# Products that nobody reads beside the copies in the recurrence of an RWKV-7 scan

## The chip, the cores and the metric

The kernel runs on one core of a Trainium2 chip. The metric is the device time of one execution in microseconds, as the median of several runs. A core has a matrix engine (TensorE, in the profile PE, with its weight loads as PEld), three engines for elementwise work (VectorE or DVE, ScalarE or ACT, GpSimd or POOL), SyncE (SP), whose queue starts transfers, and DMA engines. TensorE's output goes to PSUM, from where the elementwise engines read it.

## What is computed

A two-layer encoder on 256 tokens and 16 learned ones ahead of them, 1024 features, with 32-bit products. Layer 0 is differential attention and a dense SwiGLU; layer 1 an RWKV-7 time mixing in both directions and a SwiGLU with eight experts, of which each token takes two. The change concerns the scan of layer 1, cut here from the reference:

```python
def _wkv7_step(S, inp):
    r, w, k, v, kk, a = inp
    sa = jnp.einsum('bhvk,bhk->bhv', S, kk)
    S = S * w[:, :, None, :] - sa[..., None] * (kk * a)[:, :, None, :] + v[..., None] * k[:, :, None, :]
    y = jnp.einsum('bhvk,bhk->bhv', S, r)
    return S, y
...
_, y_fwd = lax.scan(_wkv7_step, S0, (r_t, tm(decay[0]), tm(kd[0]), v_t, kk_t, tm(a[0])))
_, y_bwd = lax.scan(_wkv7_step, S0, (r_t, tm(decay[1]), tm(kd[1]), v_t, kk_t, tm(a[1])), reverse=True)
...
out = ((y + bonus.reshape(B, L, D)) * g).astype(x.dtype)
return jnp.einsum('bld,de->ble', out, w_o)
```

There are 16 heads of 64 features; the state S of a head is 64x64.

## The kernel before

The scan is computed in chunks of 64 tokens, four chunks in each direction. The 16 heads go as eight pairs (f = 0 to 7); one head of a pair lies in the lower 64 partitions (LO), the other in the upper 64 (HI). For each pair these parts run, in `rwkv`:

- `rv` (L718) projects the pair's r and v. `prep` (L764 on) makes the decays, the rates and the matrices between the tokens of a chunk: X, TK, GA. `inverse` (L913 on) solves a triangular system for each of the eight chunks: 15 rounds on VectorE over 16x16 blocks (a shuffle L930, a product L931, a sum L932), then two levels of products (L946, L953, L967, L978, L980); its result is TF. `values` (L906) sets in the values.
- `chain` (L986 on) is the recurrence. A start (L1011 to L1020) takes the 16 learned tokens; then come four steps, i = 0 to 3, each with forward chunk i and backward chunk 3 - i. A step: products of X with the state R to slot 0 of a PSUM tile `pc` (L1028) and to the result `py` (L1032); a copy W of slot 0 on ScalarE (L1037); scaled states Zk on ScalarE (L1042); products of TF with W to slot 1 (L1045); copies of slot 1 to R, half of each direction on ScalarE (L1048) and half on VectorE (L1049); products of TK with R to slot 2 (L1054, not in step 3) and of GA with R to `py` (L1056); and on VectorE the next state from slot 2 and Zk (`state`, L1005 or L1007, not in step 3). A step needs the state of the step before it.
- `norm` (L1063 on) normalizes `py`, turns it (L1082) and multiplies by the gate, which gives gT. `out_proj` (L1171) multiplies gT with the output weights; the products of pairs 0 to 5 and the residual stand in the last two pairs, each tied behind a named product of the recurrence (the list `order`).

A tile `pc` has slots 0 to 3 of 64 columns for each direction: `psum.tile([128, 2, 4, 64], F32, name=f"pc{f % 2}", bufs=1)`, so pairs of even and odd number have one each, of one PSUM bank. Slot 3 is unused.

The order of the instructions of an engine is set by a scheduler, from the order of the program, the dependences, its own estimate of durations and priorities; the recurrence is programmed under a raised priority (`CHAIN_PRIORITY = 100`). Preparation and inverses of later pairs are set around the recurrence of an earlier one, and the last step of a pair can share its time with the first of the next. Where an instruction reads a PSUM tile that another engine has written, it waits for that engine. After the scan come a norm, the router and the experts, which stream their weights from memory.

Of the kernel before, what the change touches and what calls it, by code (L numbers as in the profile page):

```python
# [29 lines left out]
RANKS = (0, 5, 1, 2, 6, 3, 4, 7)  # L30
PLACES = {'W': 128, 'N': 64}
NL = 7
# [62 lines left out]
class Trunk:  # L95
# [193 lines left out]
    def attention(self, ap_, psum, xT, xh, xl, oh, ol, fill):  # L289
# [30 lines left out]

        raws, W = {}, {}

        def weights(h, i):
            if h % 2 == 0:
                raws[i] = self.load(w_in, 0, NF, i * D + h * 128, 256, 3 * D)
            c0 = (h % 2) * 128
            W[h, i] = self.parts(raws[i][:, :, c0:c0 + 128])

# [3 lines left out]
        def project(h, i, ks):  # L332
            if ks[0] == 0:
                S[h][i] = psum.tile([128, T], F32, name="pj", bufs=2)
            wh, wl = W[h, i]
            for k in ks:
# [271 lines left out]
    def projections(self, lp):  # L608
# [5 lines left out]
        temp = lambda f: pool.tile([128, T], F32, name="ln_q", bufs=LQ) if f % 2 else None  # L614
        W = []

        def weights(c):
            raw = self.load(I['rw_w_rkv'], D, NF, c * 256, 256, D)
            W.extend(self.parts(raw[:, :, j * 128:j * 128 + 128]) for j in range(2))

# [122 lines left out]
    def scan_consts(self, sp):  # L743
# [14 lines left out]
        for t in self.BK + self.X[0:2]:  # L758
            nc.vector.memset(t, 0.0)

    def bank(self, psum, tag="pi"):
        return psum.tile([128, 512], F32, name=tag, bufs=1 + (tag == "pa"))

# [222 lines left out]
    def chain(self, sp, psum, f, S):  # L986

        nc = self.nc
        xm, rm, R, tkm = self.xm[f % 3], self.rm[f % 2], S['R'], S['tkm']
        LO, HI = slice(0, 64), slice(64, 128)  # L990
        heads = ((0, LO), (1, HI))
        pend = S['pend']
        Zk = [None, None]
        S['order'] = order = []

        def steps():
            ps = psum.tile([128, 2, 4, 64], F32, name=f"pc{f % 2}", bufs=1)
            return [ps[:, d] for d in range(2)]

        def state(d, c, pc, keep):  # L1000

            for h, s in heads:
                e = pend[s, d, keep:keep + 1]
                if Zk[d] is None:
                    nc.vector.tensor_scalar(R[s, c, d, h, :], pc[s, 2, :], e, None, op0=OP.mult)  # L1005
                else:
                    nc.vector.scalar_tensor_tensor(R[s, c, d, h, :], pc[s, 2, :], e, Zk[d][s], op0=OP.mult, op1=OP.add)  # L1007


        pc = steps()[0]  # L1010
        nc.tensor.matmul(pc[LO, 0, :], xm[HI, 0, 0:64], rm[HI, 0, :], start=True, stop=True)  # L1011
        nc.tensor.matmul(pc[HI, 0, :], xm[LO, 1, 64:128], rm[LO, 1, :], start=True, stop=True)
        wm = sp.tile([128, 64], F32, name="wm", bufs=1)
        nc.scalar.copy(wm, pc[:, 0, :])
        for s in (LO, HI):
            nc.tensor.matmul(pc[s, 1, :], S['Tm'][s, :], wm[s, :], start=True, stop=True)
        nc.scalar.copy(rm[LO, 0, :], pc[LO, 1, :])
        nc.vector.tensor_copy(rm[HI, 1, :], pc[HI, 1, :])
        for h, s in heads:
            nc.tensor.matmul(pc[s, 2, :], tkm[:, h, :], rm[:, h, :], start=True, stop=True)  # L1020
        state(0, 0, pc, 4)
        py = self.bank(psum, f"py{f % 2}")[:, :256].rearrange("p (c j) -> p c j", c=4)
        for i in range(4):
            cs = (i, 3 - i)
            pcs = steps()
            for d in range(2):
                for h, s in heads:
                    nc.tensor.matmul(pcs[d][s, 0, :], S['X'][d][:, cs[d], 192 * h:192 * h + 64], R[:, cs[d], d, h, :],  # L1028
                                     start=True, stop=True)
            for d in range(2):  # L1030
                for h, s in heads:
                    last = nc.tensor.matmul(py[s, cs[d], :], S['X'][d][:, cs[d], 64 + 64 * h:128 + 64 * h], R[:, cs[d], d, h, :],  # L1032
                                            start=i == 0 and d == 0, stop=False)
            order.append(last)
            W = sp.tile([128, 2, 64], F32, name="W")
            for d in range(2):
                nc.scalar.copy(W[:, d, :], pcs[d][:, 0, :])  # L1037
            for d in range(2):
                if i < 3 and (i or not d):
                    Zk[d] = sp.tile([128, 64], F32, name=f"Zk{d}")  # L1040
                    for h, s in heads:
                        nc.scalar.activation(Zk[d][s], R[s, cs[d], d, h, :], AF.Copy, scale=pend[s, d, cs[d] - d:cs[d] - d + 1])  # L1042
            for d in range(2):
                for h, s in heads:
                    last = nc.tensor.matmul(pcs[d][s, 1, :], S['TF'][:, 4 * d + cs[d], h, :], W[:, d, :], start=True, stop=True)  # L1045
            order.append(last)
            for d in range(2):
                nc.scalar.copy(R[LO, cs[d], d, 0, :], pcs[d][LO, 1, :])  # L1048
                nc.vector.tensor_copy(R[HI, cs[d], d, 1, :], pcs[d][HI, 1, :])  # L1049
            for d in range(2):  # L1050
                c = cs[d]
                if i < 3:
                    for h, s in heads:
                        nc.tensor.matmul(pcs[d][s, 2, :], S['TK'][d][:, c, h, :], R[:, c, d, h, :], start=True, stop=True)  # L1054
                for h, s in heads:
                    last = nc.tensor.matmul(py[s, c, :], S['GA'][d][:, c, h, :], R[:, c, d, h, :], start=False, stop=i == 3 and d == 1)  # L1056
            order.append(last)
            if i < 3:
                for d in range(2):
                    state(d, cs[d] + 1 - 2 * d, pcs[d], cs[d] - d)  # L1060
        return py
# [454 lines left out]
    def moe(self, ep, psums, scanp):  # L1516
# [3 lines left out]
        with tc.tile_pool(name="wsp", bufs=WS) as self.wsp, ExitStack() as ps:  # L1520
# [5 lines left out]
            ring = [chunk(self.wraw, n=2048)] * 3  # L1526
            once = [chunk(mp, m, n, bufs=1) for m, n in (("ymoe", 2048), ("hth", FT), ("htl", FT), ("xe1", 2048))]
            self.raws = chain(first[:-1], once[1:3], first[-1:], once[:1], ring[:2], once[3:], ring[2:], cycle(first + ring))
            psums.close()
            psum = ps.enter_context(tc.tile_pool(name="moep", bufs=1, space=PSUM))  # L1530
# [205 lines left out]
```

## Time and profile before

| | us |
|---|---|
| median of 3 runs | 1870.36 |
| lowest and highest | 1864.54 and 1871.2 |
| profiled execution | 1868.09 |
| its span on the core | 1866.0 |
| TensorE busy in the span | 1704.3 |
| VectorE busy in the span | 1275.7 |
| scan, from the first start to the last R copy | 551 to 859.3 |

The rows are of one execution. A row of the timeline has the start, the time, the engine, the line, the operation with its names, and how many instructions it merges; in brackets stands how long the engine had been idle and what released it. A 64-wide product of 32-bit numbers is two records (passes) of TensorE. The granted clock (PEclk) is a share of full speed, 2.4 GHz; 0.50 is 1.2 GHz.

### The profile page before, as it was taken

Reading aid. Unit: us, or ns where it says so; the run is one execution under the profiler, and the core shown is the slowest. Engines: PE = TensorE matmul, PEld = TensorE weight load, DVE = VectorE, ACT = ScalarE, POOL = GpSimd, SP = SyncE. Lnnn points to the kernel's source line nnn. Section 1 sums busy time; section 2 is a strip of 40 time slices with the busy share of each in tenths; the row PEclk is TensorE's granted clock in tenths of the full one; section 3 lists DMA queues with packets and bytes.
Section 4 is the critical chain, followed back from the end, with each engine's and each line's share of the span. In section 5 each row is a group of like instructions: output and inputs, shape, how many; then the busy total and the mean of one; then the engine's idle time right before and its main releaser. Section 6 shows DMA issues by size and latency. Waiting matters only on the chain.

```text
span 1866.0 us, 30513 instructions
## 1 busy us (share of the span) xinstructions
PE 1704.3 (91%) x11422; PEld 1362.5 (73%) x11422; DVE 1275.7 (68%) x2135; ACT 912.2 (49%) x1612; POOL 624.8 (33%) x551
## 2 busy tenths in 40 slices
PE   6998999987988888897999999999999999999995
PEld 6887999975666666676986567888856668888542
DVE  6885755587868886854896446989934469899332
ACT  5665444455335335533674235766723356777210
POOL 4233100166545544512353112544501125445101
PEclk9999999988878878897999999999999999999998
DMA  6331555531101000355769899998999999999991
GB/s 210 112 114 46 179 171 178 173 102 47 57 24 53 24 24 2 131 204 207 245 235 347 347 425 426 425 343 306 341 357 353 422 420 350 322 326 348 395 388 78
DMA packets 130737, 431.79 MB, mean 231 GB/s; under 512 B 13689, under 2 KB 78674, under 8 KB 130578
## 3 DMA queue, kind: packets, MB, share of 16 engines
q1 hardware_dynamic: 127202, 427.78, 61.4%
q10 hardware_dynamic: 3376, 1.95, 0.4%
q8 instruction: 92, 1.51, 0.3%
q14 instruction: 67, 0.55, 0.1%
HBM read 428.66 MB, written 1.05 MB: 230 GB/s over the span
## 4 chain that ended last, share of the span: by engine, by line
PE 36%; issue 5%; DVE 4%; DMA 3%; POOL 1%; ACT 1%; SPq 0%; DVEq 0%; POOLq 0%; ACTq 0%
PE pgu L1414 14%; PE pgu L1429 6%; PE pd L135 3%; PE pdn L1478 3%; PE pd L136 3%; PE pd L134 3%; DVE w_lo L127 2%; DMA w_raw<-in_moe_w_down_dram 1%; POOL w_lo L127 1%; DMA w_raw<-in_moe_w_up_dram 1%; DMA w_raw<-in_moe_w_gate_dram 1%; DVE hid L1610 1%; PE pd L1508 1%; PE pt L1359 1%; PE pt L1445 1%
## 5 line engine op out<-in xcount | busy, mean ns | idle before, releaser
L127 DVE TENSOR_TENSOR w_lo<-w_raw,w_hi 128x896 fp32r<-128x896 f32 (+2 forms) x445 | 648.8, 1497 | 152.4 <-ACT w_hi L124 145.3
L124 ACT CAST w_hi<-w_raw 128x896 fp32r<-128x896 f32 (+2 forms) x580 | 537.2, 960 | 277.1 <-PE pd L136 70.9
L127 POOL TENSOR_TENSOR w_lo<-w_raw,w_hi 128x1024 fp32r<-128x1024 f32 (+1 forms) x135 | 335.3, 2484 | 624.1 <-ACT w_hi L124 476.3
L1414 PE MATMUL pgu<-w_hi,xe 128*128 128x448 f32 x1280 | 299.6, 369 | 2.4 <-DVE hid L1610 1.6
L1414 PEld LDWEIGHTS pgu<-w_hi,xe 128*128 128x128 f32 x1280 | 237.4, 188 | 26.7 <-issue 6.5
L1414 PE MATMUL pgu<-w_lo,xe 128*128 128x448 f32 x640 | 164.5, 369 | 4.7 <-DVE w_lo L127 4.6
L1429 PE MATMUL pgu<-w_raw,xs 128*64 128x448 f32 x768 | 158.1, 544 | 0.0
L1414 PEld LDWEIGHTS pgu<-w_lo,xe 128*128 128x128 f32 x640 | 118.5, 188 | 18.9 <-DVE w_lo L127 8.1
L135 PE MATMUL pd<-w_lo,hth 128*128 128x512 f32 (+1 forms) x320 | 121.3, 384 | 10.0 <-DVE w_lo L127 6.3
L136 PE MATMUL pd<-w_hi,htl 128*128 128x512 f32 (+1 forms) x320 | 119.7, 375 | 0.0
L1429 PEld LDWEIGHTS pgu<-w_raw,xs 128*64 128x64 f32 x768 | 59.1, 136 | 81.0 <-issue 76.9
L134 PE MATMUL pd<-w_hi,hth 128*128 128x512 f32 (+1 forms) x320 | 101.3, 376 | 4.1 <-ACT w_hi L124 4.1
L135 PEld LDWEIGHTS pd<-w_lo,hth 128*128 128x128 f32 x320 | 62.3, 195 | 28.9 <-DVE w_lo L127 8.3
L1478 PE MATMUL pdn<-w_raw,hth 128*64 128x512 f32 (+1 forms) x384 | 79.6, 542 | 0.0
L134 PEld LDWEIGHTS pd<-w_hi,hth 128*128 128x128 f32 x320 | 58.9, 194 | 17.3 <-ACT w_hi L124 5.7
L136 PEld LDWEIGHTS pd<-w_hi,htl 128*128 128x128 f32 x320 | 62.1, 194 | 10.2 <-issue 0.7
L134 PE MATMUL pj<-xh,w_hi 128*128 128x272 f32 x192 | 58.5, 305 | 9.8 <-ACT w_hi L124 4.9
L1478 PEld LDWEIGHTS pdn<-w_raw,hth 128*64 128x64 f32 x384 | 32.5, 137 | 37.8 <-issue 30.4
L136 PE MATMUL pj<-xh,w_lo 128*128 128x272 f32 x192 | 56.7, 295 | 0.6 <-DVE w_lo L127 0.6
L135 PE MATMUL pj<-xl,w_hi 128*128 128x272 f32 x192 | 56.5, 294 | 0.0
L1618 DVE TENSOR_TENSOR hid<-hid,pgu 64x896 f32<-64x896 f32 x12 | 13.0, 1091 | 62.3 <-ACT hid L1616 62.3
L153 POOL COPY ln_s<-ln_y 128x272 f32<-128x272 f32 x2 | 0.8, 412 | 156.2 <-DVE ln_y L150 156.2
(634 smaller groups left out, 3570.6 us busy)
## 6 DMA issues: line engine op xcount, KB each, us to landing
w_raw<-in_moe_w_down_dram SPq DMA_DIRECT2D x128, 896.0 KB, 7.5
w_raw<-in_moe_w_gate_dram SPq DMA_DIRECT2D x126, 896.0 KB, 7.3
w_raw<-in_moe_w_up_dram SPq DMA_DIRECT2D x126, 896.0 KB, 6.9
w_raw<-in_attn_w_in_dram SPq DMA_DIRECT2D x12, 1024.0 KB, 9.3
w_raw<-in_rw_w_rkv_dram SPq DMA_DIRECT2D x12, 1024.0 KB, 5.0
w_raw<-in_ffn_w_gate_dram SPq DMA_DIRECT2D x11, 1024.0 KB, 6.9
w_raw<-in_ffn_w_up_dram SPq DMA_DIRECT2D x11, 1024.0 KB, 5.3
w_raw<-in_ffn_w_down_dram SPq DMA_DIRECT2D x8, 1024.0 KB, 5.3
```

Source lines behind the costliest of these rows:

```text
L124: nc.scalar.copy(hi, raw)
L127: self.parted = eng.tensor_tensor(lo, raw, hi.bitcast(F32), op=OP.subtract)
L134: mm(ps, wh, xh, start=start, stop=False)
L135: mm(ps, wh, xl, start=False, stop=False)
L136: return mm(ps, wl, xh, start=False, stop=stop)
L1359: nc.tensor.matmul(ps[:, j, :], self.h3[:, t, 128 * f:128 * f + 128], G['og'][:, t, :], start=t == 0, stop=t == 1)
L1414: mm(ps[a][:, b, :448], xe[:, x, k, :], w[:, 448 * b:448 * b + 448], start=k == 0 and i == 0, stop=k == NF - 1 and i == 2)
L1429: self.tc.keep_in_program_order(self.nc.tensor.matmul(ps[a][64 * h:64 * h + 64, b, :448], xs[:, k, :], raws[h][:, o:o + 448], start=k == 0 ...
L1445: nc.tensor.transpose(pt[:, j, :], s[:, i0 + j:FT:NB], self.ident)
L1478: self.tc.keep_in_program_order(self.nc.tensor.matmul(pd[64 * q:64 * q + 64, c:c + n], h[:, i, :], raw[:, o:o + n], start=first and i == 0 ...
L1508: nc.tensor.matmul(ps, os, x, start=i == 0, stop=i == len(Y[q]) - 1)
L1610: nc.vector.tensor_tensor(cols(a), cols(a), pu[a][:, :, :448], op=OP.mult)
```

## The change

A helper `warm` issues n products of the constant identity matrix with itself, 64 columns wide, into a place in PSUM. Each step's `pc` tile gives its unused slot, of direction 1, lower half, as that place. Four such products are programmed behind the products with X, ahead of the copy W, and eight behind the products with GA, ahead of the next state (none in step 3). That is 8 x (4 x 4 + 3 x 8) = 320 products, 640 passes. Nothing reads them.

```diff
--- before.py
+++ after.py
@@ -758,6 +758,11 @@
         for t in self.BK + self.X[0:2]:
             nc.vector.memset(t, 0.0)
 
+    def warm(self, ps, n):
+
+        for _ in range(n):
+            self.nc.tensor.matmul(ps, self.ident[:, 0:ps.shape[0]], self.ident[:, 0:ps.shape[1]], start=True, stop=True)
+
     def bank(self, psum, tag="pi"):
         return psum.tile([128, 512], F32, name=tag, bufs=1 + (tag == "pa"))
 
@@ -992,9 +997,11 @@
         pend = S['pend']
         Zk = [None, None]
         S['order'] = order = []
+        spare = []
 
         def steps():
             ps = psum.tile([128, 2, 4, 64], F32, name=f"pc{f % 2}", bufs=1)
+            spare[:] = [ps[LO, 1, 3, :]]
             return [ps[:, d] for d in range(2)]
 
         def state(d, c, pc, keep):
@@ -1032,6 +1039,7 @@
                     last = nc.tensor.matmul(py[s, cs[d], :], S['X'][d][:, cs[d], 64 + 64 * h:128 + 64 * h], R[:, cs[d], d, h, :],
                                             start=i == 0 and d == 0, stop=False)
             order.append(last)
+            self.warm(spare[0], 4)
             W = sp.tile([128, 2, 64], F32, name="W")
             for d in range(2):
                 nc.scalar.copy(W[:, d, :], pcs[d][:, 0, :])
@@ -1055,6 +1063,7 @@
                 for h, s in heads:
                     last = nc.tensor.matmul(py[s, c, :], S['GA'][d][:, c, h, :], R[:, c, d, h, :], start=False, stop=i == 3 and d == 1)
             order.append(last)
+            self.warm(spare[0], 8 if i < 3 else 0)
             if i < 3:
                 for d in range(2):
                     state(d, cs[d] + 1 - 2 * d, pcs[d], cs[d] - d)
```

Behind the helper all lines of the scan move: L1028 is L1035 in the changed kernel, L1032 L1039, L1037 L1045, L1045 L1053, L1049 L1057, L1054 L1062, L1056 L1064, L1005 and L1007 L1012 and L1014, L930 to L932 L935 to L937, L1171 L1180, and the new products are L764. The scheduler sets the whole order anew, so other instructions move too. Three places follow.

TensorE in a step of the last pair, before (`pi` is the output projection, `pc` and `py` are the tiles of the step):

```order
L1032 MATMUL py_9207<-R,X_4978 64x64 x2
L1032 MATMUL py_9207<-R,X_4979 64x64
L1028 MATMUL pc_9281<-R,X_4978 64x64 x2
L1028 MATMUL pc_9281<-R,X_4979 64x64 x2
L1032 MATMUL py_9207<-R,X_4979 64x64
L1171 MATMUL pi<-w_raw,gT 128x256 x2
L1045 MATMUL pc_9281<-W,w_raw 64x64 x4
L1171 MATMUL pi<-kT,gT 128x256
L1056 MATMUL py_9207<-R,GA 64x64 x3
```

and in the changed kernel, with the new products at L764:

```order
L1039 MATMUL py_9487<-R,X_4979 64x64
L1035 MATMUL pc_9585<-R,X_4978 64x64 x2
L1035 MATMUL pc_9585<-R,X_4979 64x64 x2
L1039 MATMUL py_9487<-R,X_4979 64x64
L764 MATMUL pc_9585<-blob_61 64x64
L1180 MATMUL pi<-w_raw,gT 128x256
L764 MATMUL pc_9585<-blob_61 64x64
L1180 MATMUL pi<-w_raw,gT 128x256
L764 MATMUL pc_9585<-blob_61 64x64 x2
L1053 MATMUL pc_9585<-W,w_raw 64x64 x4
L1180 MATMUL pi<-kT,gT 128x256
L1064 MATMUL py_9487<-R,GA 64x64 x3
```

Four new products stand between the products with R and those with W, among the passes of the output projection, and before the next step eight more stand behind the products with TK and GA. The copy W and the state wait for the last of them.

TensorE at the seam of pairs 6 and 7, before: the start of pair 7 (L1011 to L1020) and its first step, `pc_9208`, stand behind the last products of pair 6, `py_8982`:

```order
L1056 MATMUL py_8982<-R,GA 64x64 x4
L1171 MATMUL pa<-kT,gT 128x256 x2
L1171 MATMUL pf<-kT,gT 128x256 x2
L906 MATMUL pi<-blob_61,vT 64x64 x10
L1011 MATMUL pc_9194<-rm_4973,xm 64x64
L1082 MATMUL pc_9129<-blob_61,Y 64x64 x8
L1012 MATMUL pc_9194<-rm_4973,xm 64x64
L1016 MATMUL pc_9194<-wm,Tm 64x64 x2
L1020 MATMUL pc_9194<-rm_4973,tkm 64x64 x2
L1032 MATMUL py_9207<-R,X_4978 64x64
L1028 MATMUL pc_9208<-R,X_4978 64x64 x2
L1028 MATMUL pc_9208<-R,X_4979 64x64 x2
```

and in the changed kernel, where `py_9222` and `pc_9370` belong to step 3 of pair 6, and `py_9487` and `pc_9488` to step 0 of pair 7:

```order
L1035 MATMUL pc_9370<-R,X_4976 64x64 x2
L1035 MATMUL pc_9370<-R,X_4977 64x64 x2
L1039 MATMUL py_9222<-R,X_4977 64x64
L764 MATMUL pc_9370<-blob_61 64x64
L1180 MATMUL pa<-kT,gT 128x256
L1039 MATMUL py_9487<-R,X_4978 64x64
L1035 MATMUL pc_9488<-R,X_4978 64x64 x2
L1035 MATMUL pc_9488<-R,X_4979 64x64 x2
L1039 MATMUL py_9487<-R,X_4978 64x64
L1039 MATMUL py_9487<-R,X_4979 64x64 x2
L764 MATMUL pc_9488<-blob_61 64x64 x4
```

Both steps now stand within each other. The same holds at the seams of pairs 2 and 3 and of 3 and 4; in the kernel before, the seams 0/1, 1/2, 5/6 and in part 4/5 were like this already.

VectorE around the state behind step 2 of pair 5 (`pc_8702` before), beside the inverse of pair 7 (`TD`, `inv_b`; the last number of a shape tells the round: 128x9x15 is the last):

```order
L1049 COPY R<-pc_8702 64x64
L932 TENSOR_TENSOR TD<-TD,inv_b 128x9x5
L930 STREAM_SHUFFLE inv_b<-TD 128x9x6
L931 TENSOR_TENSOR inv_b<-inv_b,QD 128x9x6
L1018 COPY rm_4972<-pc_8969 64x64
L1007 SCALAR_TENSOR_TENSOR R<-pc_8702,pend,Zk_8714 64x64 x2
L1007 SCALAR_TENSOR_TENSOR R<-pc_8702,pend,Zk_8717 64x64 x2
L932 TENSOR_TENSOR TD<-TD,inv_b 128x9x6
L1005 TENSOR_SCALAR R<-pc_8969,pend 64x64 x2
L930 STREAM_SHUFFLE inv_b<-TD 128x9x7
L931 TENSOR_TENSOR inv_b<-inv_b,QD 128x9x7
L932 TENSOR_TENSOR TD<-TD,inv_b 128x9x7
```

and in the changed kernel, where that state reads `pc_8926`:

```order
L1057 COPY R<-pc_8926 64x64
L937 TENSOR_TENSOR TD<-TD,inv_b 128x9x14
L1025 COPY rm_4972<-pc_9209 64x64
L935 STREAM_SHUFFLE inv_b<-TD 128x9x15
L1057 COPY R<-pc_8926 64x64
L936 TENSOR_TENSOR inv_b<-inv_b,QD 128x9x15
L937 TENSOR_TENSOR TD<-TD,inv_b 128x9x15
L1012 TENSOR_SCALAR R<-pc_9209,pend 64x64 x2
L947 STREAM_TRANSPOSE inv_s<-T_9101 128x512
L1014 SCALAR_TENSOR_TENSOR R<-pc_8926,pend,Zk_8942 64x64 x2
L1014 SCALAR_TENSOR_TENSOR R<-pc_8926,pend,Zk_8945 64x64 x2
```

Before, the state stood within round 6 of that inverse; now it stands behind round 15. On SP's queue two loads of expert weights pass one load of the output weights; behind the scan a few neighbours change places.

## Rows read from the trace of the kernel before

**Rows 1.** The page's head:

```profile
span 1866.0 us, 30513 instructions
```

**Rows 2.** The chain of waits that ended last, of 700 to 900 us:

```profile
0 pieces in order of time: start us, us, what
```

**Rows 3.** Engines by stretch: stretch, length, busy times, granted clock, DMA share, GB/s:

```profile
core 0: us, PE busy (x) PEld busy (x) DVE busy (x) ACT busy (x) POOL busy (x), PEclk, DMA share, GB/s
...
551.00:796.90 245.90, 207.73 (x2534) 161.72 (x2534) 195.41 (x674) 111.52 (x354) 118.00 (x193) 0.83 0.14 49
796.90:859.30 62.40, 59.26 (x659) 46.67 (x659) 27.32 (x107) 21.30 (x76) 5.27 (x8) 0.87 0.41 161
...
680.00:690.00 10.00, 9.83 (x87) 8.24 (x88) 9.47 (x38) 2.22 (x8) 5.69 (x10) 0.50 0.00 0
```

**Rows 4.** Timeline of 849.6 to 855.4 us, a step of pair 7:

```profile
850.03 0.28 PE L1056 MATMUL py<-R,GA 128*64 128x64 f32 x2
...
850.24 1.23 DVE L1007 SCALAR_TENSOR_TENSOR R<-pc,pend,Zk 64x64 f32<-64x64 f32 x4 [0.56 <-PE pc L1054]
...
851.62 0.45 PE L1028 MATMUL pc<-R,X 128*64 128x64 f32 x8
...
852.11 0.33 ACT L1037 COPY W<-pc 128x64 f32<-128x64 f32 x2
...
852.12 1.13 PE L1171 MATMUL pi<-w_raw,gT 128*128 128x256 f32 x4
...
853.18 0.45 PE L1045 MATMUL pc<-W,w_raw 128*64 128x64 f32 x8
...
854.75 0.45 PE L1054 MATMUL pc<-R,TK 128*64 128x64 f32 x8
...
855.25 0.28 DVE L1007 SCALAR_TENSOR_TENSOR R<-pc,pend,Zk 64x64 f32<-64x64 f32 x1 [0.56 <-PE pc L1054]
```

**Rows 5.** Timeline of 834 to 848.5 us, the start of pair 7:

```profile
834.79 0.33 PE L1011 MATMUL pc<-rm,xm 64*64 64x64 f32 x2 [0.94 <-DVE rm L909]
...
836.86 0.33 PE L1016 MATMUL pc<-wm,Tm 64*64 64x64 f32 x4 [0.67 <-ACT wm L1014]
...
837.75 0.48 PE L1020 MATMUL pc<-rm,tkm 128*64 128x64 f32 x4 [0.56 <-DVE rm L1018]
...
838.61 0.47 PE L1032 MATMUL py<-R,X 128*64 128x64 f32 x2 [0.38 <-DVE R L1005]
...
839.02 0.70 PE L1028 MATMUL pc<-R,X 128*64 128x64 f32 x8
...
846.40 1.84 PE L1171 MATMUL pi<-w_raw,gT 128*128 128x256 f32 x4
```

**Rows 6.** Timeline of TensorE, one pass by itself at full clock:

```profile
813.27 0.22 PE L1056 MATMUL py<-R,GA 128*64 128x64 f32 x1
```

**Rows 7.** Waits in the scan: us in total, times, longest:

```profile
ACT W L1037 <- PE pc L1028: 15.5, 12, 5.1
...
DVE R L1007 <- PE pc L1054: 6.9, 7, 2.7
DVE gsm L875 <- PE pa L874: 6.8, 3, 3.0
```

**Rows 8.** Timeline of 634 to 638.5 us, a state in the first part:

```profile
635.19 0.45 PE L1054 MATMUL pc<-R,TK 128*64 128x64 f32 x8
...
638.02 0.59 DVE L1007 SCALAR_TENSOR_TENSOR R<-pc,pend,Zk 64x64 f32<-64x64 f32 x2
```

**Rows 9.** Groups of VectorE in the scan: count, busy us, mean ns, idle before:

```profile
L932 DVE TENSOR_TENSOR TD<-TD,inv_b 128x9 f32<-128x9 f32 (+14 forms) x90 | 27.1, 301 | 2.3
L931 DVE TENSOR_TENSOR inv_b<-inv_b,QD 128x9 f32<-128x9 f32 (+14 forms) x90 | 25.5, 284 | 2.4
...
L930 DVE STREAM_SHUFFLE inv_b<-TD 128x9 f32<-128x9 f32 (+14 forms) x90 | 22.2, 247 | 0.8
```

## The prediction

> **What bounds the kernel now.** I read first the page's head, then the chain of waits, then the stretches by engine, then single steps. The profiled execution took 1868.09 us, 2.1 us of it outside its span [rows 1], and lies 2.3 us under the median of the three runs (1870.36). The chain that ended last has no piece in 700 to 900 us [rows 2]: it begins in the experts, which need the router and so the result of the last head pair. The scan stands before that, from 551 to 859.3 us, and what makes it longer or shorter moves the rest one to one. It has two parts [rows 3]. In the first 245.9 us VectorE works 195.4 us and TensorE 207.7: recurrence, preparation of later pairs and the inverses run side by side, neither engine is full, and the recurrence waits now for one, now for the other. In the last 62.4 us TensorE works 59.3 and VectorE 27.3: the recurrence of pairs 6 and 7 and the output projection (L1171) share a nearly full TensorE. The granted clock is 0.83 and 0.87 there. In single microseconds it stands at 1.00 or 0.50, so about (1 - 0.83) x 2 = 34% of the first part, 83.6 us, ran at the lower level (1.2 GHz), such as 680 to 690 us.
>
> One step of the last pair is 5.0 us [rows 4]: state (L1007) at 850.24, products with R, copy W at 852.11, products with W at 853.18, R copies, TK products at 854.75, next state at 855.25. Between the copy W and the products that read it TensorE does four passes of L1171, so this wait is no hole in this part. Holes stand only at the start of pair 7 [rows 5], 0.94, 0.67, 0.56 and 0.38 us, and the clock is low behind them: eight passes L1028 take 0.70 us at 839.02 against 0.45 at 851.62, four of L1171 1.84 at 846.40 against 1.13 at 852.12 [rows 4, 5].
>
> **The price of a spare product.** A product is two passes of 64 columns. No such product exists before, so the nearest rows bound it. Passes that alternate between the two halves cost (0.45 - 0.22) / 7 = 0.033 us each; the second pass to the same half adds 0.28 - 0.22 = 0.06 [rows 4, 6]. All spares write the same 64 partitions, so I take 0.06, or 0.12 us a product: 0.48 us for the four, 0.96 for the eight, 38.4 us for all 320. The ends are 21 us (0.033) and, at the lower clock with the ratio 0.70 / 0.45, 60 us. Nobody reads them, but they lie in the PSUM tile of their step: the changed program's copy W waits for the last of the four and the state for the last of the eight. So they do not run during the copy; they stand ahead of it. Behind the copy W wait ACT's Zk copies, and behind the state whatever VectorE has queued.
>
> The Trainium skill, PSUM — Partial Sum Buffer, section "PSUM bank collisions raise a hardware error", asks that PSUM be guarded by bank and quadrant and not by address, so a copy may not pass a matmul to other columns of its bank. The changed order agrees; no run here shows a collision. Were the guard by address, the felt share of the spares in the first part below would be near 0 instead of 9.4.
>
> **The last 62.4 us.** 84 of the spares stand here (4 for step 3 of pair 5, 40 each for pairs 6 and 7). TensorE is full, so they count in full: 84 x 0.12 = +10.1 (at 0.033 a pass 5.5). The change also lets step 0 of pair 7 share a step with step 3 of pair 6. By path alone that would save a whole step; but the output projection that fills those steps stays and TensorE has no room, so only the holes go: 0.94 + 0.67 + 0.56 + 0.38 = -2.5. If the clock no longer falls at 838, the 9.6 us to 848.2 shrink by a ratio of about 0.63 (0.45 / 0.70 and 1.13 / 1.84): -3.5. The other low stretch of this part, (1 - 0.87) x 2 x 62.4 - 10 = 6 us, would give 2.3 by the same ratio; I take half, -1.2. Sum: **+2.9**; ends about -2 (cheap spares, both falls gone) and +12 (clock as before, one hole left).
>
> **The first 245.9 us.** 236 spares, 28.3 us.
> - What of them is felt: the state waited for the TK products 7 times of 24, the copy W for its products 12 times of 32 [rows 7]; elsewhere VectorE or ACT came later than TensorE. At 635.19 the TK products begin, 0.45 us long, and the state runs at 638.02 [rows 8]: 2.4 us of slack for 0.96 of spares. I take a third: +9.4 (0 to 28.3).
> - The inverse of pair 7: ten of its fifteen rounds (L930 to L932) stood behind state 2 of pair 5 on VectorE and now stand ahead of it. A round is (27.1 + 25.5 + 22.2) / 90 = 0.83 us [rows 9], ten are 8.3. VectorE is idle a fifth of this part, spread in small pieces; I take half on the path: +4.1 (0 to 8.3).
> - Two further seams (pairs 2/3 and 3/4) share a step. 20 serial steps lie in this part, 12.3 us each, of which VectorE works 9.8 (195.4 / 20). Its work stays, so a step less saves its idle 2.5: 2 x -2.5 = -5 (0 to -25).
> - The clock: TensorE is busy 84% of the 83.6 us at the lower level, 70 us, which at the ratio 0.63 would be 44: 26 us less of TensorE's work. VectorE is late as often as not, so a third of that would be felt, 8.7; that most falls go, not all, makes it -7 (0 to -26).
>
> Sum: **+1.5**. The transfers move little (on SP's queue two expert loads pass one load of the output weights, with DMA share 0.14 in this part [rows 3]): 0. If the loads were late, the first product of the output projection would wait, and 62.4 us of work stand behind it.
>
> **Forecast.** +2.9 + 1.5 = +4.4 on 1868.09 is 1872.5. It is set against a median that stands 2.3 above this execution, but whose own runs spread over 6.7 us; I say 1873. A difference under 0.5% (9.35 us) is about what a measurement of this kernel can't tell from no change.
>
> **Rivals.**
> 1. Slower: the spares as a new wait in every step. In the first part they are felt in full where the VectorE work between R copies and state no longer covers TensorE's answer; it decides once that cover falls under the 0.96 us of the eight. For it: 12 copies W and 7 states wait for TensorE already, and rounds of pair 7's inverse, which could have served as cover behind state 5.2, move ahead. Against: slack of 2.4 us as in [rows 8]. Price: 28.3 + 10.1 - 2.5 + 4.1 - 5 = +35, with no gain from the clock: about 1903; with two thirds felt 1894. Chance 0.27.
> 2. Faster: the clock stays up. TensorE has more passes around each wait, and neither part runs at 1.2 GHz. Last part: 10.1 - 2.5 - 3.5 - 2.3 = +1.8. First part, if all 26 us are felt, since VectorE itself waits for preparation products in slow stretches (L874's 6.8 us in three waits, [rows 7]): -26 + 9.4 + 4.1 - 5 = -17.5. Together -15.7, 1852; with the seams worth more, 1840. Against: the falls come in waits for R copies and for rm [rows 5], and no spare stands there; the spares are done before the copy starts. Chance 0.23.
> The Trainium skill, TensorE: Matmul & The Clock Gate, section "HAM oscillation — how this bites in real kernels", says that a kernel whose bursts of matmuls are parted by waits has its clock taken back in each wait and starts every burst slow. The low clock behind the holes of [rows 5] agrees; by that rule alone the outcome would be this rival's 1852.
> 3. The change does not do what it says: it adds passes, the falls stay where they are, and the spares hide behind VectorE and in the new seams. Last part 10.1 - 2.5 = +7.6, first part -5 + 4.1 + a little, near +7 together or less: 1866 to 1876. Chance 0.08, within 0.5%.
>
> **How the numbers follow.** The forecast has 0.42, its own range 1860 to 1885: 0.05 of it lies above and 0.05 under the 0.5%. Faster 0.23 + 0.05 = 0.28, slower 0.27 + 0.05 = 0.32, same 0.32 + 0.08 = 0.40. For 8 in 10 the range reaches into both rivals, to rival 2's 1852 and a little under, and past the two thirds of rival 1: 1850 to 1897. It is no wider since TensorE's extra work is bounded at 38.4 us at the upper clock, and the freed time at 26 + 6.
>
> **What would show it.** In the profile after: 640 passes more on TensorE at L764, mean distance 0.06 us; copies W that start right behind the last of four, and states behind the last of eight; a last part with no hole at the start of pair 7 and 62 to 67 us long; granted clock over 0.87 in the first part and near 1.00 in the last; DVE's waits for the TK products up from 7 to about 12, by under 1 us each. I am wrong if the clock in the first part is over 0.95 with a scan under 295 us (rival 2), or if the waits of state and copy W grow by 20 us and more in sum (rival 1); also if the last part shortens by more than 2 us, which would mean that TensorE's rate there, not its passes, was the limit.

## The result, and the profile after

The changed kernel takes 1885.26 us in the median of four runs (1883.59 to 1887.04), against 1870.78 for the kernel before in the same comparison; the ratio is 1.0097, with a 95% interval of 1.0073 to 1.0121. It is slower, by 0.7% to 1.2%. The forecast of 1873 was no change; the range of 1850 to 1897 holds the time, and it lies at the very upper end of the forecast's own 1860 to 1885.

The profiled execution took 1886.28 us, its span is 1884.1, 18.1 more than before [rows 1]. The page's head and its group of the new products (lines, engine, count, busy us, mean ns):

```profile
span 1884.1 us, 31806 instructions
PE 1733.3 (92%) x12062; PEld 1390.2 (74%) x12062; DVE 1280.1 (68%) x2135; ACT 913.5 (48%) x1612; POOL 631.3 (34%) x551
...
L764 PE MATMUL pc<-blob 128*64 128x64 f32 x640 | 59.4, 245 | 0.0
```

The 640 passes are there. The scan now ends at 876.8 us instead of 859.3, and behind it nothing changed by more than a microsecond. The engines by stretch in the changed kernel, with the cut at the state behind step 2 of pair 5, as in [rows 3]:

```profile
core 0: us, PE busy (x) PEld busy (x) DVE busy (x) ACT busy (x) POOL busy (x), PEclk, DMA share, GB/s
...
551.00:811.30 260.30, 236.99 (x3027) 190.38 (x3028) 207.08 (x716) 112.98 (x356) 120.63 (x196) 0.86 0.17 60
811.30:876.80 65.50, 63.60 (x816) 49.88 (x811) 19.25 (x68) 20.73 (x74) 3.78 (x6) 1.00 0.29 102
```

The last part grew from 62.4 to 65.5 us, the first from 245.9 to 260.3: most of the loss is in the first part, though 1.1 of its 14.4 us pass before the first state has ended (552.5 us, before 551.4). VectorE has 11.7 us more to do there (207.08 against 195.41), most of it the pulled-ahead inverse of pair 7: in the last part it has 8.1 less (19.25 against 27.32). The granted clock rose in both parts, from 0.83 to 0.86 and from 0.87 to 1.00, and the kernel is slower all the same. The waits that answer to [rows 7], us in total, times, longest:

```profile
ACT W L1045 <- PE pc L764: 24.3, 17, 6.3
...
DVE R L1014 <- PE pc L764: 16.4, 10, 2.8
```

Copy W and state no longer wait for the products that they read but for the new ones behind them; 15.5 + 6.9 = 22.4 us became 40.7. What such a wait is made of shows a step of the last pair, in the timeline of the changed kernel:

```profile
864.50 0.45 PE L1035 MATMUL pc<-R,X 128*64 128x64 f32 x8
...
865.00 0.70 PE L1180 MATMUL pi<-w_raw,gT 128*128 128x256 f32 x2
865.63 0.33 PE L764 MATMUL pc<-blob 128*64 128x64 f32 x2
865.89 0.70 PE L1180 MATMUL pi<-w_raw,gT 128*128 128x256 f32 x2
866.52 0.45 PE L764 MATMUL pc<-blob 128*64 128x64 f32 x4
867.00 0.33 ACT L1045 COPY W<-pc 128x64 f32<-128x64 f32 x2 [2.13 <-PE pc L764]
...
868.95 0.45 PE L1062 MATMUL pc<-R,TK 128*64 128x64 f32 x8
869.24 0.28 PE L1064 MATMUL py<-R,GA 128*64 128x64 f32 x2
869.45 1.13 PE L1180 MATMUL pi<-kT,gT 128*128 128x256 f32 x4
870.51 1.15 PE L764 MATMUL pc<-blob 128*64 128x64 f32 x16
871.70 1.23 DVE L1014 SCALAR_TENSOR_TENSOR R<-pc,pend,Zk 64x64 f32<-64x64 f32 x4 [2.80 <-PE pc L764]
```

The products with R start at 864.50; before, the copy W came 0.49 us behind them (851.62 to 852.11, [rows 4]), now it comes at 867.00, 2.5 us behind. It waits not only for the four new products, half a microsecond, but for the passes of the output projection that stand between them in TensorE's queue. Those used to run beside the copy. The same at the state: the TK products start at 868.95, the state at 871.70, 2.75 us later where it was 0.50 (854.75 to 855.25).

### The profile page after: what moved, and what is told of

It reads as the page before. It is cut to its first block, busy times and chain, and to the rows that moved or that the text cites. A ratio compares the mean times of both kernels' runs of the same rounds, so it can differ in the third digit from the quotient of the medians.

```text
span 1884.1 us, 31806 instructions
## 1 busy us (share of the span) xinstructions
PE 1733.3 (92%) x12062; PEld 1390.2 (74%) x12062; DVE 1280.1 (68%) x2135; ACT 913.5 (48%) x1612; POOL 631.3 (34%) x551
## 3 DMA queue, kind: packets, MB, share of 16 engines
q1 hardware_dynamic: 127202, 427.78, 61.1%
HBM read 428.66 MB, written 1.05 MB: 228 GB/s over the span
## 5 line engine op out<-in xcount | busy, mean ns | idle before, releaser
L1423 PEld LDWEIGHTS pgu<-w_lo,xe 128*128 128x128 f32 x640 | 118.5, 188 | 18.8 <-DVE w_lo L127 8.1
L134 PE MATMUL pj<-xh,w_hi 128*128 128x272 f32 x192 | 58.6, 305 | 12.5 <-ACT w_hi L124 5.1
L764 PE MATMUL pc<-blob 128*64 128x64 f32 x640 | 59.4, 245 | 0.0
L764 PEld LDWEIGHTS pc<-blob 128*64 128x64 f32 x640 | 50.7, 157 | 6.5 <-issue 5.0
```

The lines of the kernel that those rows point to most:

```text
L134: mm(ps, wh, xh, start=start, stop=False)
L764: self.nc.tensor.matmul(ps, self.ident[:, 0:ps.shape[0]], self.ident[:, 0:ps.shape[1]], start=True, stop=True)
L1423: mm(ps[a][:, b, :448], xe[:, x, k, :], w[:, 448 * b:448 * b + 448], start=k == 0 and i == 0, stop=k == NF - 1 and i == 2)
```

## The experiments

Each engine's queue can be held to a given order: between every two neighbours of the wanted order a dependence is set that orders the issue and waits for nothing. So the new products and the new order, which came together, can be taken apart. All runs below but `before` and `after` are held in this way; the kernel before held to its own order was not run, so what the hold itself costs is known only together with an order.

```diff
+def in_order(tc):
...
+    dep = mybir.DependencyInfo(mybir.DependencyClass.NoSync, mybir.DependencyReason.DATA)
+    for name, text in ORDER.items():
...
+        for a, b in zip(places[:-1], places[1:]):
+            tc.add_manual_dep(mine[b], mine[a].name, dep, reason="order")
...
 def trunk(tc, I, out, dbg=None):
     Trunk(tc, I, out, dbg).build()
+    in_order(tc)
```

All times are ratios to the kernel before on the same chip, since its median differed between the three sets of runs: 1869.1 us beside order_only, spares_only, off_after and off_before, 1865.3 beside only_four, only_eight, doubled and inverse_back, 1862.2 beside the other four. Its single runs spread from 1857 to 1876 us, so one profiled execution shows where time goes, not by how much a kernel is slower to a few microseconds. "Scan" is the length from the end of the first state to the end of the last R copy in the run's one profile, "waits" the waits of copy W and state for products that stand in their PSUM tile or new ones, "clock" the granted one in the scan.

| run | new products | ratio (95%) | scan, us | waits, us | clock |
|---|---|---|---|---|---|
| before | 0 | 1 | 307.8 | 22.4 | 0.84 |
| after | 320 | 1.0097 (1.0073 to 1.0121) | 324.3 | 40.7 | 0.89 |
| order_only | 0 | 1.0002 (0.9989 to 1.0015) | 307.6 | 12.5 | 0.85 |
| spares_only | 320 | 1.0065 (1.0046 to 1.0083) | 321.5 | 51.3 | 0.88 |
| off_after | 320 | 1.0049 (1.0032 to 1.0066) | 314.2 | 15.8 | 0.91 |
| off_before | 320 | 1.0053 (1.0031 to 1.0074) | 314.8 | 20.8 | 0.89 |
| only_four | 128 | 1.0035 (1.0015 to 1.0055) | 307.9 | 34.5 | 0.86 |
| only_eight | 192 | 1.0070 (1.0039 to 1.0101) | 311.8 | 37.3 | 0.89 |
| doubled | 640 | 1.0222 (1.0193 to 1.0251) | 343.4 | 77.8 | 0.93 |
| inverse_back | 0 | 1.0012 (0.9988 to 1.0036) | 303.2 | 9.7 | 0.85 |
| best_order | 0 | 1.0019 (1.0000 to 1.0038) | 302.3 | 13.1 | 0.87 |
| holes | 256 | 1.0064 (1.0045 to 1.0082) | 313.5 | 26.5 | 0.89 |
| best_holes | 256 | 1.0086 (1.0058 to 1.0115) | 316.4 | 18.8 | 0.90 |
| first_pairs | 240 | 1.0056 (1.0036 to 1.0076) | 310.5 | 40.0 | 0.89 |

One caution goes with the table. The kernel before was traced once, in the execution of 1868.09 us. For `after` and the first set, the ratios and the differences of the scans from that trace agree within 3 us. For the eight runs of the two later sets the ratios say 5 to 9 us more than the scans. Within these sets times and scans do agree: doubled took 34 us more than only_four (scan 35.5 more), inverse_back 4.8 less (4.7 less), best_holes 13.2 more than best_order (14.1 more). So in the later sets the kernel before was faster than its one trace lets expect, and no trace shows where. Differences between runs of one set stand more firmly than the ratios of these eight.

**The order without the products.** The kernel before, held to the order of the changed one.

> The kernel before, without the new products, with every engine's queue in the order of the changed kernel. Theory A (the new products stand as a wait in front of the copy W and the state): the order itself costs nothing and the shared seams save, so 1855 to 1868 us. Theory B (the new order costs: the inverse of pair 7 ahead of the last states of pair 5, a norm ahead of states): 1880 to 1887, as the changed kernel. Theory C (the clock): the granted clock in the scan stays at 0.84 and the time says nothing on it.

The ratio is 1.0002: as a whole, and held in this way, the order costs nothing and saves nothing. Theory B, that it makes the loss, is out. Theory A's gain from the shared seams is not there either; where it went is read below.

**The products without the order.** The changed kernel, held to the order of the kernel before.

> The changed kernel with every queue in the order of the kernel before; the new products stand right behind the product that is programmed ahead of them. Theory A: slower than before by the felt part of 38 us, without the seams' gain: 1885 to 1900. Theory B: within 5 us of before, 1866 to 1876. Theory C: if the products keep the clock up and this is worth more than their wait, 1850 to 1865.

1.0065, or 12 us of the 18 by which the changed kernel is slower: in the old order, too, the products make most of the loss. The time of 1881.6 us is a little under theory A's 1885 to 1900.

**The products where nobody waits for them.**

```diff
-            self.nc.tensor.matmul(ps, self.ident[:, 0:ps.shape[0]], self.ident[:, 0:ps.shape[1]], start=True, stop=True)
+            self.nc.tensor.matmul(ps, self.ident[:, 0:ps.shape[0]], self.ident[:, 64:128], start=False, stop=False)
...
-            self.warm(spare[0], 4)
+            self.warm(py[LO, cs[0], :], 4)
...
-            self.warm(spare[0], 8 if i < 3 else 0)
+            self.warm(py[LO, cs[0], :], 8 if i < 3 else 0)
```

> The changed kernel in its own order, but the new products add zero (columns 64 to 127 of the identity against columns 0 to 63) to the open sums of py, which neither the copy W nor the state reads; the result stays what it was. Same passes on TensorE at the same places. Theory A: the waits for them go, 1860 to 1872. Theory B: 1880 to 1887. Theory C alone: like the changed kernel in its clock (0.89 in the scan).

> The kernel before in its own order with the new products added to the open sums of py (adding zero), each right behind the product programmed ahead of it: passes on TensorE, but nobody waits for them. Theory A: 1868 to 1878 (only TensorE's time). Theory B: 1866 to 1874. Theory C: the granted clock in the scan rises from 0.84 to 0.89 or more and the time falls to 1850 to 1865.

1.0049 and 1.0053. In the changed order the waits fall from 40.7 to 15.8 us and the ratio from 1.0097 to 1.0049, with intervals that do not touch: the wait is about half of the loss. In the order before, the two ratios (1.0065 and 1.0053) cannot be told apart, though the scan of the profile is 6.7 us shorter; there the copy W also waits 8.4 us, in three times, for products that write `py`, which the column "waits" leaves out. The other half of the loss stays when nobody waits: theory A alone is wrong by it. In off_after nearly all of that half stands in the last part, where TensorE is busy 60.85 of 61.30 us: from the state behind step 2 of pair 5 the last part takes 61.3 us against 55.3 in order_only, the first 252.8 against 252.4. In off_before it is spread, 3.6 us in the first part and 3.3 in the last. Products that nobody waits for, in the first part alone, were not run. Theory C's condition is met, 0.91 and 0.89, and the time did not fall. The scan's rows in off_after, with its two parts, and in off_before, with its last part:

```profile
559.90:874.00 314.10, 289.57 (x3829) 232.30 (x3829) 223.59 (x778) 132.88 (x429) 122.86 (x200) 0.91 0.20 71
559.90:812.70 252.80, 228.72 (x3043) 184.16 (x3043) 205.51 (x715) 112.04 (x355) 119.07 (x194) 0.89 0.17 62
812.70:874.00 61.30, 60.85 (x790) 48.13 (x788) 18.08 (x63) 20.84 (x74) 3.79 (x6) 1.00 0.30 109
...
554.30:869.10 314.80, 284.35 (x3830) 230.40 (x3829) 222.54 (x779) 132.03 (x430) 123.12 (x201) 0.89 0.20 71
...
804.70:869.10 64.40, 61.04 (x817) 49.79 (x816) 26.25 (x103) 21.32 (x76) 5.28 (x8) 0.97 0.40 152
```

**Four, eight, twice as many.** In the order before; the diff changes the two counts only.

> Order of the kernel before; only the four new products ahead of the copy W (128 in all, 15 us of TensorE), none ahead of the state. If TensorE's time alone counts, in proportion to the passes, a good third of the 12.5 us of all 320: +5, 1874. If the wait of the copy W is the costly one: +8 to +10, 1877 to 1879. If the state's wait is: +2 or less.

> Order of the kernel before; only the eight new products ahead of the state (192 in all, 23 us of TensorE). In proportion to the passes: +7.5, 1876.5. If the copy W's wait is the costly one: +2 to +4. If the state's is: +10 to +12, 1879 to 1881.

> Order of the kernel before; eight new products ahead of the copy W and sixteen ahead of the state, 640 in all, 77 us of TensorE at full clock. If their time is felt in proportion: twice 12.5, +25, 1894. If slack still takes part of the first ones and none of the second: +35 to +45, 1904 to 1914. If the higher clock pays more as passes are added: under +15, below 1884.

Four alone cost 0.35%, eight alone 0.70%, which their intervals allow to be the ratio of their passes (128 to 192); neither place is shown to be the costly one by itself. The waits went where the products stood: to the copy W in only_four (27.3 us), to the state in only_eight (21.1). Their sum, 1.05%, is above the 0.65% of both, which was measured in the first set; the intervals and the caution above allow it. Twice the products cost 2.22%, 41 us, against 12 for the single dose; by the scans, 35.6 against 13.7. Of the 38 us of passes in the second dose 22 (scans) to 29 us (ratios) are felt, of the same in the first 12 to 14: slack takes less of the second dose. The clock went the other way. Scan and waits of doubled:

```profile
547.70:891.10 343.40, 314.75 (x4470) 262.41 (x4469) 221.78 (x779) 132.77 (x430) 121.52 (x201) 0.93 0.18 65
...
ACT W L1045 <- PE pc L764: 44.1, 21, 9.0
...
DVE R L1014 <- PE pc L764: 33.7, 18, 3.3
```

At 0.93, the highest clock of all runs, this is the slowest kernel.

**Where TensorE really waits.** Eight products behind those with W, where TensorE waits for the R copies, adding to `py` so that nobody waits for them; in the order before, and in that of best_order.

```diff
-            self.warm(spare[0], 4)
...
             order.append(last)
+            self.warm(py[LO, cs[0], :], 8)
             for d in range(2):
                 nc.scalar.copy(R[LO, cs[d], d, 0, :], pcs[d][LO, 1, :])
...
-            self.warm(spare[0], 8 if i < 3 else 0)
```

> Order of the kernel before; eight new products in every step (256 in all, 31 us of TensorE) behind the products with W, where TensorE waits for the R copies, adding zero to open sums of py, so that neither W nor the state waits for them. If the waits for the R copies cover them and the clock pays: 1855 to 1865, clock over 0.89 in the scan. If their time is felt as that of the others (0.027 us for each of the 320 in off_before): +7, 1874 to 1876.

> The eight products of the run holes in the order of the run best_order. If a higher clock helps in the denser order: 3 to 8 us under best_order. If the products only cost: 5 to 10 us over it.

1.0064 and 1.0086. best_holes took 13.2 us more than best_order, above the 5 to 10 expected for mere cost. Put into the wait itself, the products raise the clock as much (0.89, 0.90) and cost no less. The idea of paying with idle time of TensorE fails even there.

**Only pairs 0 to 5.**

```diff
-            self.warm(spare[0], 4)
+            self.warm(spare[0], 4 if f < 6 else 0)
...
-            self.warm(spare[0], 8 if i < 3 else 0)
+            self.warm(spare[0], 8 if i < 3 and f < 6 else 0)
```

> Order of the kernel before; four and eight new products as in spares_only, but none in pairs 6 and 7, where the output projection fills TensorE. By the traces of spares_only the first part grows by 8.9 us and the last by 4.8: if that split holds, 1874 to 1878 (+9). If the cost sits in the full last part: +2 to +4.

1.0056, 10 us, as expected if the first part carries most of the cost. In the trace the first part is 5.4 us longer than in the kernel before (252.1 against 246.7) and the last 2.8 shorter (58.3 against 61.1), so the scan grows by 2.7 only. The cost is thus not a matter of the full last part alone when copy W and state wait; how much the first part has of it, 5 us or 10, the run leaves open.

**Pieces of the order.** No new products. In inverse_back the inverse of pair 7 stands behind the last states of pair 5 again, in an order that still shares the seams; best_order joins the shortest stretches of the traces.

> No new products; the changed kernel's order up to the first state of pair 5, then the order of the kernel before up to the last state of pair 6, then the changed kernel's again. So the inverse of pair 7 stands again behind the last states of pair 5, while the three shared seams stay. If the inverse ahead is what eats the seams' gain: 1852 to 1860 (order_only less 8 to 14 us). If it costs nothing: 1865 to 1869, as order_only.

> No new products. The order of the kernel before up to state 1 of pair 2, then the changed kernel's up to the first state of pair 5 (with its shared seams 2/3 and 3/4), then again that of the kernel before up to the last state of pair 6, then the changed kernel's. If the stretches of the traces add up: 103.0 + 114.3 + 42.5 + 35.6 = 295 us of scan against 307.8, so about 1855. If a gain in one stretch is given back in the next: 1865 to 1869.

Neither beats the kernel before: 1.0012 and 1.0019, with intervals that begin at 0.9988 and 1.0000. Their scans are 4.6 and 5.5 us shorter in the one profile each, which the ratios do not bear out; the caution above holds for both. The traces do show how a gain is given back, in us of the scan (ends of states):

| stretch | before | order_only | inverse_back | best_order |
|---|---|---|---|---|
| to state 2 of pair 2 | 115.4 | 123.7 | 123.6 | 123.5 |
| to state 0 of pair 3 (seam 2/3) | 36.5 | 15.6 | 16.0 | 15.6 |
| to state 0 of pair 5 (seam 3/4) | 79.0 | 85.4 | 85.5 | 85.4 |
| to state 2 of pair 5 | 15.8 | 27.6 | 17.0 | 16.8 |
| to state 2 of pair 6 | 26.2 | 28.9 | 25.5 | 25.6 |
| to the last R copy (seam 6/7) | 35.0 | 26.4 | 35.5 | 35.5 |

The shared step at seam 2/3 is worth 21 us where it stands, and 8 are lost ahead of it and 6 behind it, presumably where the work that used to lie beside a step of its own is done. best_order took its first 103 us from the order before; its next state, which ended 12.4 us later there, came 21.5 later, so the 8 were merely paid in that place. And the inverse of pair 7 costs 10.6 us ahead of state 2 of pair 5 (27.6 against 17.0) but makes the shared seam 6/7 pay: put back, it costs 9.1 at the end (35.5 against 26.4). There the start of pair 7 ends 9.9 us behind state 2 of pair 6 (829.3 after 819.4), and the last step of pair 6, which shares with it, is held up too; in order_only the start ends 0.8 behind (829.6 after 828.8).

## Why the prediction was right or wrong

The range held. The sign of the likeliest case did not: by the bound of 0.5% this is slower, which had 0.32. That the time is inside owes much to the width of the range, 47 us, since two terms of the sum failed in the same direction. Step by step:

**Price of a product: right.** Sixteen passes of L764 take 1.15 us at 870.51; less the 0.22 of the last [rows 6] that is 0.93 / 15 = 0.062 us a pass against the 0.06 taken. The doubt about 0.033 was needless.

**The guard by tile: right.** Copy W and state wait for the last new product. What the prediction did not see is that other passes would stand between the new ones, so that the wait is longer than the products (2.5 us for 0.5 us of them at 867.00). Its own rows of the changed order showed that, L1180 between four rows of L764.

**The last part: +2.9 forecast, +3.1 measured**, for about the reasons given, and closer than its terms, whose errors of 1.3 and 1.2 us cancel by luck. The order alone shortens it from 61.1 to 55.2 us (end of state to last R copy; forecast -2.5, -3.5 and -1.2, together -7.2), and the products add 8.9 (64.1; forecast 10.1). What keeps the clock up there the prediction left open; order_only has 0.97 without any new product:

```profile
547.60:800.00 252.40, 216.95 (x2564) 168.95 (x2563) 207.11 (x716) 111.32 (x356) 118.52 (x195) 0.82 0.17 61
800.00:855.30 55.30, 53.25 (x629) 41.30 (x627) 18.07 (x63) 20.80 (x74) 3.77 (x6) 0.97 0.33 120
```

The holes at the start of pair 7 [rows 5] are gone in that order, and the order alone is enough. The passes alone are enough, too: in off_before, where the old order with the late start of pair 7 stays, the last part has 0.97 as well.

**The first part: +1.5 forecast, +14.4 measured** (13.4 from the end of the first state). Two terms failed.
- *The inverse*, +4.1: order_only has 27.6 us from state 0 to state 2 of pair 5 against 15.8 before, +11.8, more than the upper end of 8.3. The timeline of VectorE in order_only:

```profile
783.86 0.23 DVE L1049 COPY R<-pc 64x64 f32<-64x64 f32 x1 [0.37 <-ACT R L1048]
...
785.32 0.23 DVE L930 STREAM_SHUFFLE inv_b<-TD 128x54 f32<-128x54 f32 x1
...
787.69 0.28 DVE L930 STREAM_SHUFFLE inv_b<-TD 128x81 f32<-128x81 f32 x1
788.00 0.24 DVE L931 TENSOR_TENSOR inv_b<-inv_b,QD 128x81 f32<-128x81 f32 x1
788.16 1.22 DVE L1007 SCALAR_TENSOR_TENSOR R<-pc,pend,Zk 64x64 f32<-64x64 f32 x4
```

From the R copy to the state 4.3 us pass here, most of them rounds; in the kernel before it was 1.5 (788.71 to 790.23 in its timeline). VectorE idles a fifth of the part, but hardly in this place, so no sign is left of the half that was to be hidden. The two seams, -5, gave -6.2 up to state 0 of pair 5. And the term stood in the wrong part of the sum: the inverse and the seam 6/7 are one trade, worth little together: inverse_back without the trade and order_only with it have the ratios 1.0012 and 1.0002, with intervals that overlap.
- *The clock*, -7: the products add 7.7 us in the first part (260.1 against order_only's 252.4), where +9.4 of felt passes less 7 were forecast. Only the sum of the two is measured, so which of them was off by how much stays open. But the condition of the -7 was not met: the granted clock rose only from 0.82 to 0.86, from 36% of the time at the lower level to 28%, which is under a quarter of the falls and not most; and in the runs where it rose more (0.91, 0.93 in the scan) the time did not fall either.

In sum the order was forecast at -8.1 us with the clock of the last part, and was 0; the products at +12.5, and were +17 (16.7 in the scans of after and order_only, 0.95% in the times). These two errors, 8 and 4, make up the 12 us between 1873 and 1885.

**The rivals.** Rival 1 named a good half of the mechanism: the waits of state and copy W grew by 18.3 us against the kernel before, just under the 20 that the prediction had set as its sign, and by 28.2 against the same order without the products. Its price of +35 was too high, since only about half of the passes' 38 us is felt: per product the runs cost between 0.03 us (off_after, 0.0049 x 1868 / 320) and 0.07 (only_eight), of 0.12 us of TensorE. In doubled more is felt, 22 to 29 us of the second dose. Rival 2 is refuted for these kernels as far as they reach its condition: the clock over 0.95 in the first part, which was its sign, came in no run; 0.92 there, in doubled, brought no gain. The Trainium skill, TensorE: Matmul & The Clock Gate, section "HAM oscillation — how this bites in real kernels", says that waits between bursts of matmuls cost the clock. The rows agree, 0.84 without the new products and 0.93 with 640; what they add is that the passes which raise the clock cost more here than it returns. Rival 3 fell with the ratio.

What stays open is how much the higher clock returned. off_after ran extra passes in its first part, 28 us by the price taken, and the part was as long as that of order_only (252.8 and 252.4 us) at 0.89 instead of 0.82; whether slack or the clock paid for them, no run here separates. Open is also why the kernel before was faster in the two later sets than its trace lets expect, and with it whether best_order's shorter scan is a gain.

## What to carry to other kernels

Work that nobody reads still has readers of its place: whatever shares the PSUM tile with a value on the critical chain makes the chain wait for it, and for everything that stands ahead of it in that engine's queue. Before filling an engine's idle time to raise its clock, count what the filling costs behind it in the queue; here passes of 38 us raised the clock in the scan from 0.84 to 0.89 and the kernel became 18 us slower. And when an edit makes a scheduler set a new order, run the new order without the edit: it tells in one run which of the two is the cause.

## What was not expected of the hardware

A clock nearer to full speed came with a slower kernel in every run that added passes. And executions differ ahead of the scan, in code that TensorE has alike in these kernels (3516 or 3517 passes): the first state ends at 548.3 us in one profile and at 559.8 in another. The first of these executions lies 5.8 us under the median of its kernel, the second 4.9 above, so this stretch accounts for much of the spread there. The stretch ahead of the scan in first_pairs and in off_after:

```profile
0.00:548.30 548.30, 489.39 (x3516) 445.38 (x3517) 379.63 (x763) 276.19 (x582) 190.80 (x211) 0.95 0.37 120
...
0.00:559.90 559.90, 498.70 (x3517) 453.53 (x3517) 382.38 (x763) 276.13 (x582) 183.18 (x211) 0.93 0.37 118
```

These are nearly twelve microseconds, with the granted clock at 0.95 and 0.93. Stretches of the scan that share an order and have no new products repeated better: up to state 0 of pair 5 order_only and inverse_back have 224.7 and 225.1, and up to state 1 of pair 2 the kernel before and best_order 103.0 and 102.0.
